# Opening and gate: fewer matmuls of ones, gate chunks copied and normalised by ScalarE, four modulation columns moved

## The chip, the cores and the metric

The kernel runs on one core of one Trainium2 chip. The metric is device time in microseconds (us) of one execution, from the first to the last instruction with what lies around them. In the text PE is the matmul engine (TensorE), DVE is VectorE, ACT is ScalarE, POOL is GpSimd and SP is SyncE, which issues most of the transfers.

## The reference

What is computed is a trunk of two layers over 512 tokens with 1024 features. Every layer has two modulated sublayers; the six modulation vectors of a layer are a matrix product with the conditioning vector. The even layer is the one that the change is in:

```python
def spatial_gating(z, ln_v_g, w_sp, b_sp):
    u, g = jnp.split(jax.nn.gelu(z), 2, axis=-1)
    bsz, length, _ = g.shape
    g = g.reshape(bsz, length // CHUNK, CHUNK, A_GROUPS, A_GROUP_DIM)
    g = layernorm(g, ln_v_g.reshape(A_GROUPS, A_GROUP_DIM))
    s = jnp.einsum('gpq,bnqgc->bnpgc', w_sp, g) + b_sp.T[:, :, None]
    return u * s.reshape(bsz, length, A_W)
...
    a = spatial_gating(z, ln_v_g, w_sp, b_sp)
    b = neighborhood_attention(split_heads(q), split_heads(k), split_heads(v), kc, vc, rpb)
    y = jnp.concatenate([a, b], axis=-1) @ w_out
...
        m = (sc_c @ w_mod[l] + b_mod[l])[:, None, :]
        sh1, s1, g1, sh2, s2, g2 = jnp.split(m, 6, axis=-1)
        h = modulate(rmsnorm(x, norm_g[l, 0]), sh1, s1)
...
        x = x + g1 * y
        x = x + g2 * sq_relu_mlp(modulate(rmsnorm(x, norm_g[l, 1]), sh2, s2), w_ff1[l], w_ff2[l])
```

Everything is in 32-bit floating point. There are four chunks of 128 tokens and four groups of 128 gate features, so the gate is normalised in 16 blocks of 128x128.

## The kernel before

Weights come in tiles of 1 MB (`raw`). ACT casts each piece of a tile to a rounded high part (L148, `whi`), and DVE or POOL subtracts for the low part (L143, `wlo`). A product of a weight and an activation is then three matmuls: high by high, high by low, low by high (L88 to L90 for a block alone, L221 to L224 for two blocks in `together`). All results go to eight PSUM banks that are handed out in a ring (`bank`); a matmul that takes a bank waits until the last reader of its former content is done. Scratch tiles come from a ring of six (`slot`). Each engine executes its instructions in the order in which the code is written, so an instruction that waits holds all that stands behind it on its engine.

**Opening.** `keep_warm(n, cols)` (L403) issues n matmuls of ones into a spare bank (L406); each is two passes on PE. It is called with ten of 512 columns. Behind them PE forms the column sums of x squared (L415): ACT squares a block of x (L420), DVE adds two blocks (L422), and PE sums each pair over the partitions, four pairs in all. All later work needs these sums.

**Attention and gate.** The loop over units u of the attention goes over pairs. For a pair it writes the scores (L885; DVE adds the bias and takes the maximum in L898, ACT exponentiates in L902), the weighing of the pair before (L931, with the sums broadcast in L939, copied by ACT in L943 and multiplied by DVE in L945), and seven steps of a filler (`more`). `turn` transposes the probabilities (L915) and ACT copies them out (L917, `pt`). The filler's parts are the value tokens (transposes copied by ACT to `vtok` in L692 and L693), the projections, the gate and the spatial product:

- `gate(i)` multiplies the tokens with one weight tile, chunk by chunk, 128x256 each (L802 to L804). For each chunk `gelu2` runs: ACT squares the chunk out of PSUM (L778), DVE multiplies by it (L779), ACT applies Tanh (L781), DVE multiplies again (L782, `gn`). DVE reads the chunk in PSUM in L779 and in L782. Then come the statistics of two blocks (L815, L816).
- `gate_norm(i)` adds epsilon to eight variances (L826, `gsd`), POOL raises them to a power (L827), and two steps later eight `tensor_scalar` (L833) normalise the eight blocks: on POOL for i=0, on DVE for i=1.
- `spatial` multiplies the normalised blocks with the spatial weights (L842), and DVE adds the bias (L845).

Behind the loop the u blocks are computed: one by L88 to L90, two by `together` (L221 to L224), with their own GELU.

**Modulation columns.** A column of the modulation is one DVE instruction over 128x1024 (L596, `gemv`). It stands in a queue from which `work` takes one. Of the first 24 columns each has its half tile (512 KB) loaded by a DMA that ACT issues (`early_load`, L581); from column 24 on whole tiles of 1 MB are loaded by SP (`gemv_load`, L589). In the attention loop each pair of units takes three columns, at steps 0, 2 and 5. `more` also makes one low part of the weights at each step, on POOL (`W.pieces(1, pool)`).

**Behind the attention** the tile of x is loaded by SP (L1047) and the first residual adds `g1 * y` to it on DVE (L1051).

## Time and profile before

| | us |
|---|---|
| median of 3 runs | 1169.52 |
| lowest and highest run | 1166.28, 1169.98 |
| the profiled execution | 1169.07 |
| its span | 1167.3 |
| PE busy | 1153.0 (99%) |
| DVE busy | 721.1 (62%) |
| ACT busy | 474.0 (41%) |
| POOL busy | 163.7 (14%) |

The span runs from the first to the last instruction that the profiler recorded; the time of the execution has 1.8 us more around it. Busy is the time in which an engine executed something. PE's share of 99% means that it seldom waits; matmuls are pipelined, and it says nothing of whether each of them was needed or ran at the full clock.

### The profile page before, as it was taken

The page shows a single profiled execution, that of the slowest core. Times are in us where ns is not written, and L with a number is a line of the kernel's source. Part 1 is how long each engine was busy: PE and PEld are TensorE (multiplying, and loading weights), DVE is VectorE, ACT ScalarE, POOL GpSimd, SP SyncE. Part 2 cuts the span into 40 slices and gives each one's busy share as a digit, 9 for nine tenths or more (in the row PEclk, how much of TensorE's full clock was granted, in tenths as well). Part 3 has the DMA queues.
Part 4 walks back from the last instruction along what each step waited for, and adds up shares of the span by engine and source line. Part 5 has one row for each costly group of instructions (what it writes and reads, how often), then busy time and mean ns, then how long its engine had stood idle before and what let it go on. Part 6 is the DMA issues. An engine that isn't in the chain of part 4 may idle for free.

```text
span 1167.3 us, 16568 instructions
## 1 busy us (share of the span) xinstructions
PE 1153.0 (99%) x6620; PEld 960.2 (82%) x6620; DVE 721.1 (62%) x1257; ACT 474.0 (41%) x939; POOL 163.7 (14%) x157
## 2 busy tenths in 40 slices
PE   9999999999999999999999999999999999999997
PEld 5788888789888888888889766799888888888887
DVE  3865778758765665666667869577743443443545
ACT  4564455546431432422336232575641331331423
POOL 0051226533000000000023120143200000000001
PEclk9999999999999999999999999999999999999999
DMA  9624543351564554554541444303232232232222
GB/s 371 244 91 145 172 163 113 123 216 38 216 214 150 213 215 153 209 216 156 204 145 42 147 112 141 105 26 120 72 109 85 96 108 93 88 108 77 104 73 72
DMA packets 32333, 161.91 MB, mean 139 GB/s; under 512 B 4416, under 2 KB 8000, under 8 KB 16256
## 3 DMA queue, kind: packets, MB, share of 16 engines
q1 hardware_dynamic: 28224, 146.43, 36.0%
q10 hardware_dynamic: 4032, 14.42, 3.7%
q8 instruction: 52, 0.85, 0.3%
q14 instruction: 25, 0.20, 0.1%
HBM read 152.52 MB, written 2.10 MB: 132 GB/s over the span
## 4 chain that ended last, share of the span: by engine, by line
PE 92%; DVE 5%; ACT 2%; DMA 1%; issue 1%; ACTq 0%; DVEq 0%; POOL 0%; POOLq 0%
PE ps L88 23%; PE ps L89 23%; PE ps L90 23%; PE ps L224 4%; PE ps L221 4%; PE ps L222 4%; PE ps L1310 3%; PE ps L491 2%; PE ps L406 1%; PE ps L931 1%; DMA graw<-in_wmB_dram 1%; DVE graw L596 1%; PE ps L885 1%; PE ps L455 1%; PE ps L915 1%
## 5 line engine op out<-in xcount | busy, mean ns | idle before, releaser
L148 ACT CAST whi<-raw 128x512 fp32r<-128x512 f32 x340 | 191.5, 616 | 198.1 <-PE ps L90 145.7
L88 PE MATMUL ps<-hhi,whi 128*128 128x512 f32 x608 | 238.4, 392 | 1.4 <-DVE gn L782 1.4
L89 PE MATMUL ps<-hhi,wlo 128*128 128x512 f32 x608 | 236.7, 389 | 0.0
L90 PE MATMUL ps<-hlo,whi 128*128 128x512 f32 x608 | 236.7, 389 | 0.0
L143 DVE TENSOR_TENSOR wlo<-raw,whi 128x512 fp32r<-128x512 f32 x285 | 195.1, 721 | 33.8 <-ACT whi L148 32.8
L90 PE MATMUL ps<-hid,whi 128*128 128x512 f32 (+1 forms) x520 | 196.3, 378 | 0.0
L89 PE MATMUL ps<-hid,wlo 128*128 128x512 f32 (+1 forms) x520 | 196.3, 378 | 0.0
L88 PE MATMUL ps<-hid,whi 128*128 128x512 f32 (+1 forms) x520 | 196.3, 378 | 0.0
L1051 DVE SCALAR_TENSOR_TENSOR x<-ps,mod,x 128x512 f32<-128x512 f32 (+1 forms) x94 | 62.7, 669 | 157.5 <-PE ps L90 147.9
L143 POOL TENSOR_TENSOR wlo<-raw,whi 128x512 fp32r<-128x512 f32 x55 | 81.0, 1490 | 426.2 <-ACT whi L148 426.1
L88 PEld LDWEIGHTS ps<-hhi,whi 128*128 128x128 f32 x608 | 114.1, 188 | 28.3 <-issue 3.2
L90 PEld LDWEIGHTS ps<-hlo,whi 128*128 128x128 f32 x608 | 114.1, 188 | 23.9
L89 PEld LDWEIGHTS ps<-hhi,wlo 128*128 128x128 f32 x608 | 114.2, 188 | 22.9
L596 DVE CUSTOM_DVE_ANT_0 graw<-graw,cB,vec 128x1024 f32<-128x1024 f32 x80 | 106.1, 1328 | 16.8 <-DMA graw<-in_wmB_dram 16.8
L88 PEld LDWEIGHTS ps<-hid,whi 128*128 128x128 f32 x520 | 97.8, 188 | 18.3
L89 PEld LDWEIGHTS ps<-hid,wlo 128*128 128x128 f32 x520 | 97.8, 188 | 18.1
L90 PEld LDWEIGHTS ps<-hid,whi 128*128 128x128 f32 x520 | 97.8, 188 | 18.0
L1186 DVE TENSOR_TENSOR z<-z 128x512 f32<-128x512 f32 (+1 forms) x72 | 46.8, 657 | 93.4 <-ACT z L1184 93.3
L1184 ACT ACTIVATE z<-ps 128x512 f32<-128x512 f32 (+1 forms) x72 | 38.9, 550 | 138.5 <-PE ps L90 136.3
L1190 DVE TENSOR_TENSOR hid<-z,hid 128x512 fp32r<-128x512 f32 (+1 forms) x72 | 45.7, 641 | 43.3 <-ACT hid L1188 43.3
L1188 ACT CAST hid<-z 128x512 fp32r<-128x512 f32 (+1 forms) x72 | 40.6, 572 | 52.2 <-DVE z L1186 52.2
L1540 POOL TENSOR_TENSOR o<-o,rstd 128x256 f32<-128x256 f32 x2 | 1.9, 950 | 321.7 <-DVE rstd L362 321.7
(267 smaller groups left out, 1733.3 us busy)
## 6 DMA issues: line engine op xcount, KB each, us to landing
raw<-in_w_ff_dram SPq DMA_DIRECT2D x64, 1024.0 KB
graw<-in_wmB_dram SPq DMA_DIRECT2D x28, 1024.0 KB
graw<-in_wmB_dram ACTq DMA_DIRECT2D x24, 512.0 KB
raw<-in_w_pw_dram SPq DMA_DIRECT2D x12, 1024.0 KB
raw<-in_w_in_dram SPq DMA_DIRECT2D x8, 1024.0 KB
wmA<-in_wmA_dram SPq DMA_DIRECT2D x7, 1024.0 KB
y<-ypad SPq DMA_DIRECT2D x90, 67.5 KB
raw<-in_w_out_dram SPq DMA_DIRECT2D x4, 1024.0 KB
```

The costliest lines, as they stand in the source:

```text
L88: pe.matmul(ps, w[0], a[0], start=first, stop=False)
L89: pe.matmul(ps, w[1], a[0], start=False, stop=False)
L90: pe.matmul(ps, w[0], a[1], start=False, stop=last)
L143: (e or dve).tensor_tensor(lo.parts[q], src, hi.parts[q].bitcast(F32), op=ALU.subtract)
L148: act.copy(hi.parts[q], src)
L221: pe.matmul(ps, w[0][:, k, c : c + P], a[0], start=n == 0, stop=False)
L222: pe.matmul(ps, w[1][:, k, c : c + P], a[0], start=False, stop=False)
L224: pe.matmul(ps, w[0][:, k, c : c + P], a[1], start=False, stop=n == len(ks) - 1)
L596: dve.tensor_tensor_reduce(out=wv, in0=wv, in1=cB, scale=1.0, scalar=vcol(V_BMOD, l * 48 + q * 8 + j % 8), op0=ALU.mult, op1=ALU.add, accu ...
L1051: dve.scalar_tensor_tensor(x[:, m, t0:t1], ps, gate[:, m : m + 1], x[:, m, t0:t1], op0=ALU.mult, op1=ALU.add)
L1186: dve.tensor_tensor(z, z, z, op=ALU.mult)
L1190: dve.tensor_tensor(lo, z, hi.bitcast(F32), op=ALU.subtract)
```

## The change

**Opening.** `keep_warm` gets five matmuls in place of ten, and one more stands behind the column sums of the second pair (k = 3).

On PE at the start of the program the rows were (`ps_127` is the spare bank, `sq` the squares):

```order
L406 MATMUL ps_127<-ones 128x512 x10
L415 MATMUL ps_140<-ones,sq_143 128x128 x4
L415 MATMUL ps_140<-ones,sq_152 128x128 x4
L415 MATMUL ps_140<-ones,sq_161 128x128 x4
L415 MATMUL ps_140<-ones,sq_170 128x128 x4
L455 MATMUL ps_212<-graw_86,sc_125 32x512 x4
```

and are now:

```order
L406 MATMUL ps_127<-ones 128x512 x5
L415 MATMUL ps_135<-ones,sq_138 128x128 x4
L415 MATMUL ps_135<-ones,sq_147 128x128 x4
L406 MATMUL ps_127<-ones 128x512
L415 MATMUL ps_135<-ones,sq_157 128x128 x4
L415 MATMUL ps_135<-ones,sq_166 128x128 x4
L457 MATMUL ps_208<-graw_86,sc_125 32x512 x4
```

Five of the matmuls of ones are gone ahead of the sums, and one stands between the second and the third pair.

**Gate chunk.** ACT copies each chunk of 128x256 from PSUM into the second half of the scratch tile before it squares it; Square and both DVE multiplications then read the copy. The bank is free after ACT's copy instead of after L782.

**Normalisation.** A small DVE instruction forms `gnb`, minus mean times the power of the variance (128x8). Eight ACT activations (Identity with scale and bias by pointer, 128x128) take the place of the eight `tensor_scalar`, for both i, with the loop over e outside and over n inside. Lines shift: L692 of before is L695 now, L778 is L782, L902 is L911, L917 is L926, and the new activations are L843.

On ACT, at the first batch (around the `vtok` copies, with the first chunk of `gate(1)` ahead), the rows were:

```order
L148 CAST whi_1879<-raw_1435 128x512
L778 ACTIVATE gelu_1896<-ps_1865 128x256
L148 CAST whi_1879<-raw_1435 128x512
L692 COPY vtok_1909<-ps_1910 128x512
L693 COPY vtok_1909<-ps_1911 128x384
L943 COPY rs_1963<-ps_1954 128x512
L902 ACTIVATE s_1967,tot_1921<-s_1967,st_1968 128x512
L902 ACTIVATE s_1971,tot_1921<-s_1971,st_1972 128x512
```

and are now:

```order
L816 COPY gelu_1896<-ps_1865 128x256
L782 ACTIVATE gelu_1896<-gelu_1896 128x256
L843 ACTIVATE gn_1637<-gn_1637,gnb_1900,gsd_1862 128x128
L843 ACTIVATE gn_1730<-gn_1730,gnb_1900,gsd_1862 128x128
L843 ACTIVATE gn_1774<-gn_1774,gnb_1900,gsd_1862 128x128
L843 ACTIVATE gn_1849<-gn_1849,gnb_1900,gsd_1862 128x128
...
L148 CAST whi_1879<-raw_1431 128x512
L695 COPY vtok_1912<-ps_1913 128x512
L696 COPY vtok_1912<-ps_1914 128x384
L952 COPY rs_1966<-ps_1957 128x512
L911 ACTIVATE s_1970,tot_1924<-s_1970,st_1971 128x512
```

The eight new activations (the four rows left out have the names of the four shown) stand between the Square of the chunk and the copies to `vtok`, behind which the sums' copy and the exponentials come.

On ACT, at the second batch (last exponential of the last pair to the last copies of the probabilities), the rows were:

```order
L902 ACTIVATE s_2198,tot_1921<-s_2198,st_2199 128x512
L148 CAST whi_2149<-raw_1739 128x512
L581 DMA graw_817<-in_wmB_dram 128x1024
L148 CAST whi_2149<-raw_1739 128x512 x2
L917 COPY pt_2244<-ps_2239 128x512
L917 COPY pt_2251<-ps_2246 128x512
L581 DMA graw_817<-in_wmB_dram 128x1024
L917 COPY pt_2267<-ps_2262 128x512
L917 COPY pt_2274<-ps_2269 128x512
```

and are now:

```order
L911 ACTIVATE s_2200,tot_1924<-s_2200,st_2201 128x512
L843 ACTIVATE gn_1637<-gn_1637,gnb_2210,gsd_2141 128x128
L843 ACTIVATE gn_1730<-gn_1730,gnb_2210,gsd_2141 128x128
L843 ACTIVATE gn_1774<-gn_1774,gnb_2210,gsd_2141 128x128
L843 ACTIVATE gn_1849<-gn_1849,gnb_2210,gsd_2141 128x128
...
L148 CAST whi_2151<-raw_1737 128x512 x3
L926 COPY pt_2246<-ps_2241 128x512
L926 COPY pt_2253<-ps_2248 128x512
L926 COPY pt_2267<-ps_2262 128x512
L926 COPY pt_2274<-ps_2269 128x512
```

The eight activations (four shown) stand behind the exponentials, the two DMA issues (L581) are gone, and the three casts of the weights stand ahead of the probability copies.

**Modulation columns.** The first 20 columns instead of 24 go by half tiles. In the loop the pairs u = 12 and 14 take one column each, at step 5, in place of three. Columns 20 to 23 come behind the attention, out of whole tiles that SP loads: 20 and 21 at the last two k steps of `together` for the u blocks 2 and 3, 22 and 23 at k steps 4 and 6 of the first residual. SP issues one whole tile ahead of the loads of x.

**Low parts.** From `begin(gate_norm(1))` on, `more` makes the low parts on DVE instead of POOL.

The diff, cut to its core:

```diff
-    keep_warm(10, 512)
+    keep_warm(5, 512)
...
             column_sums(sq, k == 1, k == KC - 1)
+            if k == 3:
+                keep_warm(1, 512)
...
-    gpool = [None, 12]
+    NE = 20
+    gpool = [None, NE // 2]
...
-        if j < 24:
+        if j < NE:
             b = j % 2 * D
             act.dma_start(early[0][:, b : b + D], I["wmB"][j // 2][:, b : b + D])
...
-        if j < 22:
+        if j < NE - 2:
             soon.append([3, lambda: early_load(j + 2)])
-        elif j == 23:
+        elif j == NE - 1:
             gemv_load(gpool[1])
...
-    def gelu2(dst, ps, n):
-
-        t = slot(cols=n, s="gelu")
+    def gelu2(dst, ps, n, t=None):
+
+        if t is None:
+            t = slot(cols=n, s="gelu")
         act.activation(t, ps, AF.Square, scale=math.sqrt(0.044715))
...
-            def rest(gt=gt, ps=ps, n=n):
-                yield from gelu2(gt, ps, 256)
+            t = slot(s="gelu")
+            act.copy(t[:, 256:], ps)
+
+            def rest(gt=gt, t=t, n=n):
+                yield from gelu2(gt, t[:, 256:], 256, t[:, :256])
...
-        for n in range(4):
-            for e in range(2):
+        nb = small(8, "gnb")
+        dve.scalar_tensor_tensor(nb.rearrange("p (n e) -> p n e", e=2), gmv[:, :, 2 * i : 2 * i + 2, 0], -1.0,
+                                 sd.rearrange("p (n e) -> p n e", e=2), op0=ALU.mult, op1=ALU.mult)
+        for e in range(2):
+            for n in range(4):
                 g = 2 * i + e
-                (dve if i else pool).tensor_scalar(gn[n][:, g * P : (g + 1) * P], gn[n][:, g * P : (g + 1) * P],
-                                  gmv[:, n, g, 0:1], sd[:, 2 * n + e : 2 * n + e + 1],
-                                  op0=ALU.subtract, op1=ALU.mult)
+                act.activation(gn[n][:, g * P : (g + 1) * P], gn[n][:, g * P : (g + 1) * P], AF.Identity,
+                               scale=sd[:, 2 * n + e : 2 * n + e + 1], bias=nb[:, 2 * n + e : 2 * n + e + 1])
...
+        low_by[0] = dve
         yield from spatial((0, 1))
...
-            W.pieces(1, pool)
+            W.pieces(1, low_by[0])
...
-            if n in (0, 2, 5):
+            if n in ((0, 2, 5) if u < 12 else (5,)):
                 work(1)
...
+    queue_gemv(NE, 24)
+
+    def hook(n):
+        if 0 < n < 7:
+            operand((4, 5, 6, 7, 0, 1)[n - 1])
+        if n > 5:
+            work(1)
...
-    evs = together([(0, w, 0), (1, w, P)], y, res, ks=order, hook=lambda n: W.pieces(n % 2, "both"))
+    evs = together([(0, w, 0), (1, w, P)], y, res, ks=order,
+                   hook=lambda n: (W.pieces(n % 2, "both"), work(n in (4, 6))))
```

## Rows read from the trace of the kernel before

**Rows 1.** The page, part 4: the chain that ended last, by engine.
```profile
PE 92%; DVE 5%; ACT 2%; DMA 1%; issue 1%; ACTq 0%; DVEq 0%; POOL 0%; POOLq 0%
```

**Rows 2.** What PE waited for: line, releaser; us in total, times, longest.
```profile
PE ps L88 <- DVE gn L782: 1.4, 1, 1.4
...
PE ps L885 <- DVE gn L782: 1.0, 1, 1.0
...
PE ps L931 <- ACT pt L917: 0.7, 1, 0.7
```

**Rows 3.** Timeline of PE, opening: start, us, engine, line, operation, out<-in, count [idle <-releaser].
```profile
0.99 11.13 PE L406 MATMUL ps<-ones 128*128 128x512 f32 x20 [0.99 <-POOL expo L314]
11.96 3.73 PE L415 MATMUL ps<-ones,sq 128*128 128x128 f32 x32
```

**Rows 4.** Timeline of PE's weight loads, opening.
```profile
4.57 0.34 PEld L406 LDWEIGHTS ps<-ones 128*128 128x128 f32 x1 [0.52 <-issue]
5.42 0.29 PEld L406 LDWEIGHTS ps<-ones 128*128 128x128 f32 x1 [0.52 <-issue]
5.95 0.19 PEld L406 LDWEIGHTS ps<-ones 128*128 128x128 f32 x1 [0.24 <-issue]
6.38 0.19 PEld L406 LDWEIGHTS ps<-ones 128*128 128x128 f32 x1 [0.24 <-issue]
```

**Rows 5.** Timeline of ACT, opening.
```profile
8.63 1.67 ACT L420 ACTIVATE sq<-x 128x512 f32<-128x512 f32 x3 [0.59 <-DMA x<-in_xT_dram]
13.05 0.63 ACT L420 ACTIVATE sq<-x 128x512 f32<-128x512 f32 x1 [2.75 <-PE ps L415]
```

**Rows 6.** Timeline of DVE, opening.
```profile
9.81 0.69 DVE L422 TENSOR_TENSOR sq<-sq,sq 128x512 f32<-128x512 f32 x1 [1.04 <-ACT sq L420]
```

**Rows 7.** Windows: us, busy by engine (x instructions), PE's granted clock, DMA share, GB/s.
```profile
10.00:20.00 10.00, 10.00 (x67) 6.35 (x67) 4.24 (x13) 2.88 (x6) 0.00 (x0) 1.00 1.01 397
```

**Rows 8.** Timeline of ACT, attention: the first vtok copy.
```profile
172.50 0.59 ACT L692 COPY vtok<-ps 128x512 f32<-128x512 f32 x1
```

**Rows 9.** Timeline of DVE, attention: variance and epsilon of the first batch.
```profile
172.65 0.17 DVE L826 TENSOR_SCALAR gsd<-gmv 128x8 f32<-128x8 f32 x1
```

**Rows 10.** Timeline of POOL, attention: the two powers.
```profile
172.90 2.60 POOL L827 TENSOR_TENSOR gsd<-gsd,expo 128x8 f32<-128x8 f32 x1 [7.81 <-DVE gsd L826]
...
194.08 1.67 POOL L827 TENSOR_TENSOR gsd<-gsd,expo 128x8 f32<-128x8 f32 x1 [6.33 <-DVE gsd L826]
```

**Rows 11.** Timeline of PE, attention: first gate matmul of the second weights.
```profile
175.39 0.39 PE L802 MATMUL ps<-whi,hhi 128*128 128x256 f32 x1
```

**Rows 12.** Lines L502, L1428 on ACT, by form: ns min/median/max, first and last start.
```profile
L502 ACT ACTIVATE hhi<-x,modA,gsA x8: 800/808/819, 20.9 to 45.4; 128x512 fp32r<-128x512 f32 x8
...
L1428 ACT ACTIVATE zc<-zc,vec x16: 597/601/603, 754.6 to 777.9; 128x256 f32<-128x256 f32 x16
```

**Rows 13.** Timeline of ACT, attention: casts and probability copies.
```profile
198.28 1.65 ACT L148 CAST whi<-raw 128x512 fp32r<-128x512 f32 x3
...
204.65 1.07 ACT L917 COPY pt<-ps 128x512 f32<-128x512 f32 x2 [3.76 <-DVE mod L596]
```

**Rows 14.** Timeline of DVE, attention: the second batch.
```profile
197.67 5.31 DVE L833 TENSOR_SCALAR gn<-gn,gmv,gsd 128x128 f32<-128x128 f32 x8
```

**Rows 15.** Timeline of PE, end of the attention: first u block.
```profile
207.66 0.50 PE L88 MATMUL ps<-hhi,whi 128*128 128x512 f32 x1
```

**Rows 16.** Windows at the end of the kernel, columns as in rows 7.
```profile
1162.00:1163.00 1.00, 0.00 (x0) 0.00 (x0) 1.00 (x4) 0.00 (x0) 0.69 (x2) 0.87 0.43 133
1163.00:1164.00 1.00, 0.00 (x0) 0.00 (x0) 0.27 (x1) 0.00 (x0) 0.00 (x0) 0.50 1.00 329
```

**Rows 17.** The page, part 5: busy, mean ns | idle before, releaser.
```profile
L143 DVE TENSOR_TENSOR wlo<-raw,whi 128x512 fp32r<-128x512 f32 x285 | 195.1, 721 | 33.8 <-ACT whi L148 32.8
...
L596 DVE CUSTOM_DVE_ANT_0 graw<-graw,cB,vec 128x1024 f32<-128x1024 f32 x80 | 106.1, 1328 | 16.8 <-DMA graw<-in_wmB_dram 16.8
```

**Rows 18.** Timeline of DVE, first residual: x<-ps.
```profile
238.17 1.41 DVE L1051 SCALAR_TENSOR_TENSOR x<-ps,mod,x 128x512 f32<-128x512 f32 x2 [6.30 <-DMA x<-in_xT_dram]
```

More of the change, by code (lines that the diff above doesn't have):

```diff
@@ L594, in gemv @@
         l, q = gemv_srcs[j // 8]
-        wv = (early[0] if j < 24 else gemv_tile[i])[:, e * D : (e + 1) * D]
+        wv = (early[0] if j < NE else gemv_tile[i])[:, e * D : (e + 1) * D]
         dve.tensor_tensor_reduce(
@@ L598, in gemv @@
             op0=ALU.mult, op1=ALU.add, accum_out=mods[(l, q)][:, j % 8 : j % 8 + 1])
-        if j < 22:
+        if j < NE - 2:
             soon.append([3, lambda: early_load(j + 2)])
-        elif j == 23:
+        elif j == NE - 1:
             gemv_load(gpool[1])
             gpool[1] += 1
-        elif e and j > 23:
+        elif e and j >= NE:
             del gemv_tile[i]
@@ L961, in body @@
     early_load(1)
-    queue_gemv(0, 24)
+    queue_gemv(0, NE)
     gate_in = {}
+    low_by = [pool]
     def filling():
@@ L980, in body @@
     fill = filling()
-    nfill = [0]
     def more(n):
@@ L985, in more @@
             begun = len(staged)
-            if next(fill, 1) is None:
-                nfill[0] += 1
+            next(fill, 1)
             stage(begun)
@@ L1027, in operand @@
         split(y[k][0], y[k][1], yb[k - 4] if k > 3 else sg[k], el=pool if k % 2 else dve)
+    queue_gemv(NE, 24)
[4 more added lines that the diff above has]
+            work(1)
     w = W.use()
-    evs = together([(2, w, 0), (3, w, P)], h, evac_u, hook=lambda n: operand((4, 5, 6, 7, 0, 1)[n - 1]) if 0 < n < 7 else None)
+    evs = together([(2, w, 0), (3, w, P)], h, evac_u, hook=hook)
     W.free()
```

## The prediction

> **What bounds the kernel now.** I read the chain of waits first: PE carries 92% of it, DVE 5%, ACT 2% [rows 1]. So only what makes PE start earlier, do less or wait less can move the end. The list of PE's waits comes next, since it prices what can be had. In the attention three of its entries belong to code the change touches: 1.4 and 1.0 us for L782, where DVE reads a gate chunk out of PSUM for the last time and so keeps the bank that PE wants, and 0.7 us for the copies of the probabilities (L917) [rows 2]. That is 3.1 us. The third view is the timeline of the opening, where PE runs matmuls of ones (L406) for 11.13 us and only then reaches the column sums (L415), 32 passes in 3.73 us [rows 3]. The sums end at 15.69 and everything after hangs on them. PE is never idle there, so the list of waits can't show this cost; the timeline does.
>
> All below is in the frame of the profiled execution, 1169.07 us. The median of the runs is 0.45 above it, less than the spread of the three runs, and is left aside. About 0.3% (3.5 us) is what a measurement of this kernel can tell from no change.
>
> **Opening: fewer matmuls of ones.** One L406 instruction is two passes (x20 for ten). Their weight loads show two rates: 0.85 us apart up to 5.42, then 0.43 [rows 4]. The removed ones are the late ones, so each pass is worth 0.43, not 11.13 / 20. With five instructions the ten passes end at 12.12 - 10 x 0.43 = 7.82. A column sum takes 3.57 / 32 = 0.112 a pass (11.96 to the last start), eight for each k pair, 0.90. Walk: the sums for k=1 run 7.82 to 8.72. The sums for k=3 end at 9.66, the new instruction of ones (two passes) at 10.52. For k=5 the DVE sum is ready at 9.81 + 0.69 = 10.50 [rows 6], so PE goes on to 11.42. For k=7 the eighth Square had waited at 13.05 for PE to release its slot [rows 5]; now the slot is free when the seventh ends at 8.63 + 1.67 = 10.30. Square 0.63, DVE sum 0.69 with its start: 11.7, and PE 11.7 to 12.6, with the pipeline's tail 12.7. Against 15.69 that is **3.0 us earlier**. What could come late next is a transfer: the 16 DMA engines are full from 10 to 20 us (share 1.01) [rows 7], and the modulation weights are consumed right behind. PE waited for no DMA here before; in the worst case I give back 1.0 us of the gain, and one more pass of ones' worth (0.43) may come on top: 2.0 to 3.4.
>
> **Gate chunk copied by ACT.** The copy of 128x256 frees the bank earlier, and DVE then reads SBUF. The two waits for L782, 1.0 and 1.4 us, go. The copy lengthens a chunk's ACT to DVE chain by about 0.45 (128x512 takes 0.59 [rows 8], and shorter forms are not half).
>
> **Normalisation on ACT, the first batch.** Before, POOL did eight L833 and nobody waited long. Now eight activations stand on ACT in one row, ahead of the cast and of the two vtok copies (L692, L693), and they wait for gnb, which waits for POOL's power (L827). The engine runs in its order, so vtok waits too. And PE's first gate matmul of the next part writes the bank that the first vtok copy reads. Before, that copy ran at 172.50 [rows 8] and PE started the matmul at 175.39 [rows 11].
> Now step by step. gsd starts at 172.65 [rows 9], or up to 0.45 later. The power took 2.60 the first time and 1.67 the second [rows 10]; it starts 0.25 behind gsd. So it ends between 172.90 + 1.67 = 174.6 and 173.35 + 2.60 = 175.95; gnb adds 0.25. An L843 of 128x128 with scale and bias by pointer has no row. The nearest are the 128x512 form, 0.808, and the 128x256 form, 0.601 [rows 12]; by the line through them 128 columns take 0.50. Activations in a row overlap: three Squares of 0.63 took 1.67, so a next one starts 0.11 before the last ends, a step of 0.39. Eight: 0.50 + 7 x 0.39 = 3.2. Bounds: 2.9 with a step of 0.35, 4.0 without overlap. Then a cast, 0.5, and the copy, 0.59. The copy ends between 174.85 + 4.3 = 179.2 and 176.2 + 4.3 = 180.5; middle 179.9. PE would be there at 175.39 - 1.0 (the wait at L885 that goes) = 174.4. So **PE stands idle about 5.5 us**, and starts the gate matmul 4.5 us late (3.8 to 5.1).
>
> **How much of it reaches the end of the attention.** From there on PE had 1.4 of waiting for L782, which goes, so it comes 3.1 late to the second spatial part. The second gnb stands on DVE where the eight L833 began at 197.67 [rows 14], thus at about 200.8. ACT: eight L843 to 204.0, three casts (1.65 for three before), then four pt copies at 1.07 for two [rows 13], the last ending about 207.6. Before, it ended at 204.65 + 1.07 = 205.72, because ACT had waited 3.76 behind a modulation column. PE began the next matmul of 128x512 at 207.66, 1.94 behind that copy [rows 15]. So now 209.4: the attention ends **1.7 us later** (0.9 to 2.5). The removed L833 of DVE (5.31) and three moved columns are therefore not a gain of PE: eight activations have taken their place on ACT, and the 3.1 us of old waits are already used up in this sum.
>
> **What the idle stretch does to PE's clock.** The trace has no PE gap of 5 us with work behind it. [...] What a restart costs is shown by the opening: passes at 0.85 instead of 0.43 up to 5.42, 4.4 us at half rate, so 2.2 us lost. I take most of it, 1.7, since ACT's queue paces part of what follows; bounds 0 and 2.2.
> [...]
>
> **The rest.** Low parts of four plus four weights go from POOL to DVE. They take 0.72 each there [rows 17], and PE waited for none of these parts: nothing. The four moved columns: 20 and 21 run while PE does the 128x512 matmuls of the u blocks, and 22 and 23 lie in the 6.30 us for which DVE is idle ahead of L1051 at 238.17 [rows 18]: hidden. If that cover were gone, 1.33 each [rows 17], 2.7 us for such a pair. SP issues one more whole load ahead of the x loads; x is what ended those 6.30 us, so it could come late by the time of 1 MB. I cost it at 0, with 0.5 as the bad end, since the load is issued long before. The extra row for gnb is small (0.2).
>
> **Sum, the forecast.** 1169.07 - 3.0 + 1.7 + 1.7 = **1169.5 us**.
>
> **The rivals.** First, the stall comes but the clock stays high: 1169.07 - 3.0 + 1.7 = 1167.8. For it: in the whole trace the column of granted clock falls only at the end, after the work. Against it: there it fell as soon as PE had run dry.
> Second, the change does what its form suggests: the power and the eight activations pass quickly, or the vtok copies find slack that I don't see, so that PE doesn't stand. Then both gains come: 1169.07 - 3.0 - 3.1 = 1163.0, **faster**. Against it is the row order of ACT; for it, that the old normalisation and columns held ACT for 3.76 us, which goes.
> Third, **slower**: the clock falls in the stall and stays at half rate for more than the opening needed, since the matmuls behind it are short and come with waits for ACT. Half rate costs half of its duration. To come out beyond 1172.6 the attention must lose 6.6 us, of which 1.7 is the stall, so 4.9 by the clock, that is 10 us at half rate, 2.2 times the opening's 4.4. I put such a case at 1169.07 - 3.0 + 1.7 + 5.5 = 1173.3. Against it: the next part has some 29 us of nearly dense matmuls.
> A fourth, that the opening gives nothing because a transfer ends the wait, would put the forecast at 1172.5; I give it little and count it with the third.
>
> **How the numbers follow.** Forecast 0.40, clock stays 0.28, no stall 0.18, slower (with the fourth) 0.14. Faster by over 0.3% means below 1165.6: all of the no-stall case and some of the lower tail of the second, 0.22. Slower means beyond 1172.6: the third and a tail of the forecast, 0.16. The rest, 0.62, is within 0.3%. The range for 8 in 10 goes from 1163.5 (the forecast and the clock case with their bounds: 1169.07 - 3.4 + 0.9 = 1166.6, then into the no-stall case, of which half stays out) to 1172.5 (1169.07 - 2.0 + 2.5 + 2.2 + 0.5 = 1172.3).
>
> **What would show it.** In the new timeline: L415 ends near 12.7; if it ends near 15 the opening's step is wrong. In the attention the list of PE's waits has a gate matmul held for 5 to 6 us by the vtok copy; if no wait above 2 us stands there, the second rival is right. Matmuls of 128x256 right behind it that start twice as far apart as those of before at 175.39 would show the fall of the clock. The first matmul of the u block (207.66 before) should come, counted from the end of L415, 1.7 to 3.4 later than it did. What would make me wrong is a quicker power or L843, or DVE or PE waiting for the moved loads.

## The result and the profile after

| | before | after |
|---|---|---|
| median, us | 1169.67 (9 runs, 1166.28 to 1170.78) | 1173.3 (9 runs, 1171.94 to 1174.64) |
| ratio to before | | 1.0034, 95% interval 1.0023 to 1.0044 |
| the profiled execution, us | 1169.07 | 1172.26 |
| its span, us | 1167.3 | 1170.5 |
| PE busy, us | 1153.0 | 1151.3 |

The change makes the kernel slower by 3.6 us by the medians, 3.2 by the two profiled executions. The forecast was 1169.5, with a range up to 1172.5: about no change was expected, and the median lies 0.8 beyond the range. The profiled execution lies 1.0 below the median.

Read one after the other, the views of after show where the time went. First the opening, in PE's timeline (columns as in rows 3):

```profile
0.99 7.29 PE L406 MATMUL ps<-ones 128*128 128x512 f32 x10 [0.99 <-POOL expo L314]
8.11 1.96 PE L415 MATMUL ps<-ones,sq 128*128 128x128 f32 x16
9.91 1.02 PE L406 MATMUL ps<-ones 128*128 128x512 f32 x2
10.77 1.95 PE L415 MATMUL ps<-ones,sq 128*128 128x128 f32 x16
```

The sums end at 10.77 + 1.95 = 12.72, against 15.69 before [rows 3]: 2.97 us won, the size that was worked out. Then the list of PE's waits (line, releaser; us in total, times, longest):

```profile
PE ps L806 <- ACT vtok L695: 7.8, 1, 7.8
...
PE ps L224 <- DVE ylo L94: 0.7, 1, 0.7
```

Both waits for L782, 1.4 and 1.0 us, and the one for the probability copies, 0.7 [rows 2], are gone. In their place stands one of 7.8 us, where a gate matmul waits for the vtok copy, and a new one of 0.7 us for a low part of y. The timeline of ACT shows the first one's make-up:

```profile
170.32 0.42 ACT L782 ACTIVATE gelu<-gelu 128x256 f32<-128x256 f32 x1
175.01 3.18 ACT L843 ACTIVATE gn<-gn,gnb,gsd 128x128 f32<-128x128 f32 x8 [4.27 <-DVE gnb L838]
178.10 0.60 ACT L148 CAST whi<-raw 128x512 fp32r<-128x512 f32 x1
178.61 0.57 ACT L695 COPY vtok<-ps 128x512 f32<-128x512 f32 x1
```

After the Square (170.32) ACT is idle for 4.27 us until gnb is there, runs the eight activations in 3.18, casts, and only at 178.61 copies vtok. DVE and POOL in the same stretch, gsd and gnb on DVE, the power and a low part of the weights on POOL:

```profile
170.87 0.17 DVE L833 TENSOR_SCALAR gsd<-gmv 128x8 f32<-128x8 f32 x1
...
173.76 1.21 DVE L838 SCALAR_TENSOR_TENSOR gnb<-gmv,gsd 128x8 f32<-128x8 f32 x1 [1.19 <-POOL gsd L834]
```

```profile
171.12 2.61 POOL L834 TENSOR_TENSOR gsd<-gsd,expo 128x8 f32<-128x8 f32 x1 [7.74 <-DVE gsd L833]
173.70 1.26 POOL L143 TENSOR_TENSOR wlo<-raw,whi 128x512 fp32r<-128x512 f32 x1
```

And PE's timeline when it is released, with the slices of 3 us around it (columns as in rows 7; the granted clock is the third column from the end):

```profile
179.23 0.58 PE L806 MATMUL ps<-whi,hhi 128*128 128x256 f32 x1 [7.79 <-ACT vtok L695]
179.61 0.41 PE L807 MATMUL ps<-whi,hlo 128*128 128x256 f32 x1
179.82 0.41 PE L808 MATMUL ps<-wlo,hhi 128*128 128x256 f32 x1
```

```profile
172.00:175.00 3.00, 0.00 (x0) 0.00 (x0) 1.79 (x4) 0.00 (x0) 2.95 (x2) 0.79 0.04 16
175.00:178.00 3.00, 0.00 (x0) 0.00 (x0) 0.00 (x0) 2.99 (x8) 0.00 (x0) 0.50 0.00 0
178.00:181.00 3.00, 1.77 (x8) 1.77 (x9) 0.94 (x2) 2.03 (x5) 1.27 (x1) 0.50 0.00 0
181.00:184.00 3.00, 3.00 (x16) 3.00 (x16) 2.19 (x8) 2.60 (x7) 0.00 (x0) 0.50 0.01 3
184.00:187.00 3.00, 3.00 (x28) 3.00 (x27) 2.02 (x6) 2.59 (x8) 1.76 (x2) 1.00 0.17 30
```

PE is empty from 172 to 179. The granted clock is 0.79 and then 0.50 in these slices, and back at 1.00 in the one from 184. Behind the wait matmuls start 0.21 apart, and 0.12 apart once the clock is back (184.06 and 184.18). At the end of the attention the first u block starts here:

```profile
209.26 0.50 PE L88 MATMUL ps<-hhi,whi 128*128 128x512 f32 x1
```

Before, it was 207.66 [rows 15]. Counted from the end of the sums it comes at 209.26 - 12.72 = 196.54, before at 207.66 - 15.69 = 191.97: the stretch up to the end of the attention is 4.57 us longer. From there to the last matmul the changed kernel loses another 1.6 us: 1.0 at the low part of y and behind it, and 0.6 in the depthwise convolution near 742 us. The sum, -2.97 + 4.57 + 1.6 = 3.2, is the difference of the spans. All of this compares one execution of each kernel.

### The profile page after: what moved, and what is told of

Same layout as the page of the kernel before. It is cut to its first block, busy times and chain, and to the rows that moved or that the text cites. A ratio compares the mean times of both kernels' runs of the same rounds, so it can differ in the third digit from the quotient of the medians.

```text
span 1170.5 us, 16535 instructions
## 1 busy us (share of the span) xinstructions
PE 1151.3 (98%) x6612; PEld 959.1 (82%) x6612; DVE 725.2 (62%) x1259; ACT 483.1 (41%) x963; POOL 145.9 (12%) x141
## 4 chain that ended last, share of the span: by engine, by line
PE 92%; DVE 4%; ACT 2%; issue 1%; DMA 0%; POOL 0%; DVEq 0%; ACTq 0%; POOLq 0%
PE ps L88 23%; PE ps L90 23%; PE ps L89 23%; PE ps L1328 3%; PE ps L224 3%; PE ps L221 3%; PE ps L222 3%; PE ps L493 2%; PE ps L940 1%; PE ps L924 1%; PE ps L894 1%; PE ps L406 1%; PE ps L457 1%; DVE ylo L94 1%; DMA graw<-in_wmB_dram 0%
## 5 line engine op out<-in xcount | busy, mean ns | idle before, releaser
L143 DVE TENSOR_TENSOR wlo<-raw,whi 128x512 fp32r<-128x512 f32 x293 | 200.1, 720 | 37.4 <-ACT whi L148 36.5
L143 POOL TENSOR_TENSOR wlo<-raw,whi 128x512 fp32r<-128x512 f32 x47 | 69.4, 1488 | 425.3 <-ACT whi L148 423.7
L343 ACT ACTIVATE sq<-x 128x256 f32<-128x256 f32 (+1 forms) x41 | 20.3, 496 | 64.3 <-DVE x L1068 64.2
```

Of the source, the lines that this page charges most:

```text
L143: (e or dve).tensor_tensor(lo.parts[q], src, hi.parts[q].bitcast(F32), op=ALU.subtract)
```

## The experiments

Each run is timed beside the kernel before on the same chip; these stood at 1169.61, 1169.44 and 1169.86 us in the three groups. An offset is the start of a matmul in a run's timeline less the start of the same matmul in the one timeline of before; a minus sign means earlier.

### The opening alone

```diff
-    keep_warm(10, 512)
+    keep_warm(5, 512)
...
             column_sums(sq, k == 1, k == KC - 1)
+            if k == 3:
+                keep_warm(1, 512)
```

> The kernel before with the change of the opening alone. My theory: the opening gives what it did in the trace of after, where every PE instruction from the column sums to the attention starts 3.02 us earlier, and nothing downstream takes it back; so 3.0 us less than before, a ratio of 0.9974. The rival, that the gain is lost again further down because the attention or a transfer sets the end: a ratio of 1.000, with the offset against before going back to zero in the attention.

Measured: 1167.68 us, ratio 0.9985 (0.9976 to 0.9994). It is a gain, but of 1.9 us and not of 3.0. In its profile the matmuls behind the opening are 2.46 us early up to the attention and 3.04 behind it (a part of that is the wait at L887, 1.0 before as L885 and 0.65 here), and 1.2 is lost in the convolution, which leaves 1.9. So what is won in the opening is still there behind the attention; where it is lost is the convolution. The opening itself differs from one execution to the next. Timelines of PE and ACT:

```profile
8.17 2.20 PE L415 MATMUL ps<-ones,sq 128*128 128x128 f32 x16 [0.57 <-DVE sq L422]
```

```profile
6.26 2.17 ACT L420 ACTIVATE sq<-x 128x512 f32<-128x512 f32 x4
9.10 2.19 ACT L420 ACTIVATE sq<-x 128x512 f32<-128x512 f32 x4 [0.67 <-DMA x<-in_xT_dram]
```

PE now waits 0.57 us for the sum of the first pair: its matmuls of ones end sooner than in after (0.99 + 6.61 = 7.60 against 8.28), and ACT's Squares begin later, at 6.26 (after: 5.95). The second four Squares wait 0.67 us for x. With ten matmuls of ones that was hidden: PE reached the sums at 11.96. So the ones were what held the sums before, and behind them the loads of x have a say in when the opening ends.

### The first batch back on POOL

```diff
+        if i == 0:
+            for n in range(4):
+                for e in range(2):
+                    pool.tensor_scalar(gn[n][:, e * P : (e + 1) * P], gn[n][:, e * P : (e + 1) * P],
+                                       gmv[:, n, e, 0:1], sd[:, 2 * n + e : 2 * n + e + 1],
+                                       op0=ALU.subtract, op1=ALU.mult)
+            return
         nb = small(8, "gnb")
```

> The changed kernel with the first batch of the normalisation back on POOL (eight L833 as before) and only the second on ACT. My theory, that eight activations ahead of the vtok copies make the 7.8 us wait: no PE wait above 1.5 us is left in the attention, the clock stays high there, and the time falls to about 1166 to 1168 us, ratio to before 0.996 to 0.999, like the run in which the activations stand one step later on ACT. The rival, that the copies of the chunks or the low parts on DVE make the wait: a wait of 5 us or more stays and the time stays above 1171.

Measured: 1165.30 us, ratio 0.9965 (0.9953 to 0.9978): 8.0 us below the changed kernel, and 4.1 below the kernel before. What is left of PE's waits in the attention:

```profile
PE ps L947 <- ACT pt L933: 0.4, 1, 0.4
...
PE ps L806 <- ACT vtok L695: 0.3, 1, 0.3
```

Nothing above 0.4 us. So the wait of 7.8 us comes from the first batch on ACT, and everything else in the change together is a gain: 4.1 us by the medians, of which the opening alone gave 1.9.

### The first batch one step later on ACT

```diff
         yield
         yield
+        if i == 0:
+            yield
         nb = small(8, "gnb")
```

> The changed kernel with one more step between the power and the first eight activations, so that they stand on ACT behind the two vtok copies, the sums' copy and the exponentials of the next pair. My theory: the 7.8 us wait of PE is the place in ACT's row, not the work of the activations. So no PE wait above 1 us is left there, the granted clock stays at 1.00, and the attention ends earlier than in the kernel before by the 3 us of old waits or a part of them, instead of 4.6 later: 5 to 7.5 us less than the changed kernel, 1166 to 1168 us, a ratio to before of 0.996 to 0.998. The rival, that eight activations on ACT cost PE as much wherever they stand, since ACT has no room in the attention: the wait moves to the probability copies or to the spatial product, and the time stays within 1.5 us of the changed kernel's 1173.3.

Measured: 1168.11 us, ratio 0.9987 (0.9978 to 0.9996), 5.2 below the changed kernel and 0.1 above the expected stretch. The wait for vtok has shrunk to 0.3, with the same eight activations on ACT; what made the long wait was their place. But no wait above 1 us and a clock of 1.00 were expected too, and that was missed:

```profile
PE ps L926 <- ACT s L913: 2.1, 1, 2.1
...
PE ps L806 <- ACT vtok L695: 0.3, 1, 0.3
```

PE waits 2.1 us, from 191.4 to 193.5, for the exponentials of the last pair: DVE comes late to their scores. Here the clock falls too, in slices of 2 us:

```profile
192.00:194.00 2.00, 0.52 (x3) 0.52 (x4) 2.00 (x7) 1.39 (x4) 0.44 (x1) 0.88 0.00 0
194.00:196.00 2.00, 2.00 (x9) 1.90 (x8) 1.15 (x4) 2.00 (x8) 0.00 (x0) 0.50 0.03 8
196.00:198.00 2.00, 2.00 (x11) 1.59 (x11) 0.00 (x0) 2.00 (x6) 0.00 (x0) 0.77 0.00 0
```

The run with the first batch on POOL differs from this one in that batch alone. There the wait for the same exponentials is 0.3, and the time is 2.8 us lower. So of the 8.0 us that the first batch on ACT costs, 5.2 are its place, and 2.8 are left in the later place: the rival was right in a part.

### The chunk copies alone

```diff
+            t = slot(s="gelu")
+            act.copy(t[:, 256:], ps)
...
-            def rest(gt=gt, ps=ps, n=n):
-                yield from gelu2(gt, ps, 256)
+            def rest(gt=gt, t=t, n=n):
+                yield from gelu2(gt, t[:, 256:], 256, t[:, :256])
```

> The kernel before with the copy of the gate chunks by ACT alone, everything else as before. By the list of PE's waits both waits for L782 (1.0 and 1.4 us) go. If PE's waits are independent of each other: 2.4 us less than before, ratio 0.998. The rival: the chunk's chain is longer by the copy (0.4 us four times a part) and PE waits for the exponentials or the spatial product instead; the time is within 1 us of before, ratio 0.999 to 1.001.

Measured: 1169.20 us, ratio 0.9997 (0.9988 to 1.0006), no change. The two waits for L782 are gone, and in the list of PE's waits stands instead

```profile
PE ps L919 <- ACT s L906: 1.7, 1, 1.7
```

a wait for the exponentials of the last pair. In this one profile the first u block starts 1.48 us earlier than before, of which 0.45 was there ahead of the attention: 1.0 is left of the 2.4, and the medians don't show even that clear of noise. DVE, with three columns in each pair, is late to the scores anyway.

### Opening, copies and second batch, nothing moved

The kernel before with the opening's edit, the copies, and the new normalisation for i = 1 only:

```diff
+        if i:
+            nb = small(8, "gnb")
+            dve.scalar_tensor_tensor(nb.rearrange("p (n e) -> p n e", e=2), gmv[:, :, 2 * i : 2 * i + 2, 0], -1.0,
+                                     sd.rearrange("p (n e) -> p n e", e=2), op0=ALU.mult, op1=ALU.mult)
...
+            return
         for n in range(4):
             for e in range(2):
                 g = 2 * i + e
-                (dve if i else pool).tensor_scalar(
+                pool.tensor_scalar(
```

> The kernel before with the opening's change, the chunk copies, and the second batch of the normalisation on ACT; the first batch stays on POOL, all 24 columns and the low parts stay where they were. If the three add up: the opening 1.9 us (as measured alone), the copies up to 2.4, the second batch up to 0.7 for the probability copies: 1164.6 to 1166 us, ratio 0.996 to 0.997, faster than any run so far. The rival: the second batch on ACT delays the probability copies by more than the columns did (in the changed kernel they come from 205.3 on, 5 us behind the last exponential), so that the copies' gain is lost: 1167 to 1168.

Measured: 1166.05 us, ratio 0.9972 (0.9963 to 0.9982), at the upper end of the first expectation, with the wait of 1.7 us for the exponentials still there. By the ratios that is some 1.5 us below the opening alone, with all 24 columns in the loop (the intervals just overlap). Against the run with the first batch on POOL (1165.30) it lacks the moved columns and low parts; they make 0.75 us by the medians, and the intervals overlap. The profiles show why it is little. From the start of the attention to the first u block after it, this run gains 1.6 us against before, and the one with columns and low parts moved 3.1, of which 1.0 is lost again at the low part of y.

### The late batch with all 24 columns in the loop

```diff
-    NE = 20
+    NE = 24
...
-            if n in ((0, 2, 5) if u < 12 else (5,)):
+            if n in (0, 2, 5):
                 work(1)
```

(with the later calls for the four columns taken out)

> The changed kernel with the first eight activations one step later on ACT (as in the earlier run) and with all 24 columns where they were before. It tells what the move of the four columns is worth once the long wait is gone. My theory: the move costs more than it gives, since PE's wait of 0.7 us for the low part of y comes from columns 20 and 21; but three columns in each of the last pairs make DVE late to the scores of the last pair, where PE already waits 2.1 us for the exponentials. I expect about no change against 1168.1, between 1167 and 1169.5: no wait for ylo, a longer one (3 us or more) for the exponentials. The rival, that the move is a gain by itself: 1170 or more.

Measured: 1171.41 us, ratio 1.0015 (1.0006 to 1.0024). The rival was right: moving the columns is worth 3.3 us beside the late batch (1168.11 with them moved). PE's waits:

```profile
PE ps L926 <- ACT s L913: 2.3, 1, 2.3
...
PE ps L896 <- ACT pt L928: 1.9, 1, 1.9
```

The wait for the low part of y is gone, as expected, but a new one of 1.9 us for the probability copies has come, beside 2.3 for the exponentials. Behind the wait of 1.9 the granted clock is 0.59 and 0.56 in the slices from 186 to 190, so a part of the 3.3 us is the clock's. The copies start at 185.91, behind a Tanh (L785) for which ACT waits 2.6 us, until DVE has done a column (1.65 us) and the multiplication of the chunk (1.47).

### Matmuls of ones in the stretch of the wait

```diff
             pr = bank()
+            if u == 11:
+                for _ in range(8):
+                    pe.matmul(pr, ones, ones.unsqueeze(1).to_broadcast([P, 4, P]), start=True, stop=True)
```

> The changed kernel with eight more matmuls of ones (16 passes of 0.43, 6.9 us) ahead of the broadcast of the sums at the end of pair 2, which is just where PE runs dry; they write the bank that the broadcast writes next. They compute nothing that is used. PE still has to wait for the vtok copy, until the same moment, but is busy for most of the time. My theory: the clock's fall costs about 2.1 us (the offset against before grows from +3.8 to +5.9 over the gate matmuls behind the wait, at half rate). So the granted clock stays 1.00, the gate matmuls run at full rate, and the time is about 2 us less than the changed kernel's, 1171.3, a ratio to before of 1.0015. The rival: what PE loses at half rate is covered by ACT's queue, which sets the end of the attention anyway; the time stays at 1173.3 within 0.5 us.

Measured: 1172.75 us, ratio 1.0031 (1.0019 to 1.0043). That is 0.55 below the changed kernel: the 2 us of the first expectation were not there, and the rival (within 0.5) is nearer. In its profile the offset at the start of the attention is -2.15, in that of after -3.02, so the opening had won 0.9 less there. It was run again beside the changed kernel:

> The changed kernel once more, beside the two runs that are compared with it. As before: 1173.3 within 1 us, PE's wait for the vtok copy 7.8 us.

> The changed kernel with eight matmuls of ones in the stretch where PE waits for the vtok copy, beside the changed kernel itself. In the profile of the first such run the matmuls behind the wait stood 2.1 us earlier, counted from the end of the opening, and the end of the attention 1.3 us earlier. My theory, that the clock's fall costs 1.3 us of the end: 1.3 us less than the changed kernel in this comparison (0.8 to 2.1). The rival, that it costs nothing at the end: within 0.5 us.

Measured: the changed kernel 1173.12 us, ratio 1.0029 (1.0017 to 1.0040); with the ones 1172.23, ratio 1.0024 (1.0014 to 1.0034). The difference of the medians is 0.9 us, inside what was expected, and the intervals overlap, so by the times alone it is weak. The profile is plain. PE's wait for vtok, the slices from 175 to 184, and the first gate matmuls:

```profile
PE ps L806 <- ACT vtok L695: 0.7, 1, 0.7
```

```profile
175.00:178.00 3.00, 3.00 (x8) 1.09 (x6) 0.61 (x1) 2.35 (x7) 0.59 (x1) 1.00 0.00 0
178.00:181.00 3.00, 2.27 (x26) 1.98 (x26) 0.29 (x1) 2.68 (x7) 1.28 (x1) 1.00 0.00 0
181.00:184.00 3.00, 3.00 (x27) 3.00 (x26) 2.84 (x9) 1.96 (x5) 0.00 (x0) 1.00 0.03 8
```

```profile
179.88 0.39 PE L806 MATMUL ps<-whi,hhi 128*128 128x256 f32 x1 [0.73 <-ACT vtok L695]
180.10 0.28 PE L807 MATMUL ps<-whi,hlo 128*128 128x256 f32 x1
180.22 0.28 PE L808 MATMUL ps<-wlo,hhi 128*128 128x256 f32 x1
```

The release comes at the same moment (179.88; in the second run of the changed kernel 179.87), with the clock at 1.00 and matmuls 0.12 apart. The first u block then starts at 208.58 instead of 209.62 in that run: of the clock's price of 2.1 about 1.0 us reaches the end of the attention. The rest is lost where PE, now earlier, meets ACT's row: it waits 0.23 for a probability copy at 205.24, and the copies pace the matmuls behind it.

### Low parts on DVE from the first power on

```diff
         yield from gate(0)
+        low_by[0] = dve
         begin(gate_norm(0))
         yield from gate(1)
         begin(gate_norm(1))
-        low_by[0] = dve
```

> The changed kernel with the low parts of the weights on DVE from the first power on, instead of from the second, so that POOL does none while DVE forms gnb. In the changed kernel gnb took 1.21 us where a DVE instruction of 128x8 takes 0.17, with a low part of 1.26 us on POOL at the same time. My theory, that the two engines hold each other up there: gnb takes about 0.2, the activations begin 1.0 us earlier, PE's wait shrinks from 7.8 to about 6.8, and the time by 0.5 to 1.0. The rival, that gnb is slow for a reason of its own (its operands with steps of 2 and 8): gnb stays at 1.2 and the wait at 7.8 or more.

Measured: 1171.26 us, ratio 1.0014 (1.0006 to 1.0023), 1.9 below the changed kernel in the same group, twice what was expected (the two intervals overlap in part). On DVE, on POOL, and PE's wait:

```profile
173.35 0.17 DVE L838 SCALAR_TENSOR_TENSOR gnb<-gmv,gsd 128x8 f32<-128x8 f32 x1
```

```profile
171.26 2.05 POOL L834 TENSOR_TENSOR gsd<-gsd,expo 128x8 f32<-128x8 f32 x1 [7.74 <-DVE gsd L833]
```

```profile
PE ps L806 <- ACT vtok L695: 6.2, 1, 6.2
```

gnb takes 0.17 in place of 1.21, and the power 2.05 in place of 2.61. In the changed kernel POOL's low part had started at 173.70, 0.06 ahead of gnb, and gnb ended with it: 173.76 + 1.21 = 174.97, and 173.70 + 1.26 = 174.96. The wait is 6.2, which is 1.6 less; 1.0 of that is gnb's and 0.5 the power's.

### The four columns later

```diff
     def hook(n):
         if 0 < n < 7:
             operand((4, 5, 6, 7, 0, 1)[n - 1])
-        if n > 5:
-            work(1)
...
-        chunk(2 + i, w, i * P, y, res, 0, order, el="both")
+        chunk(2 + i, w, i * P, y, res, 1.2, order, el="both")
```

> The changed kernel with modulation columns 20 and 21 moved out of the last two steps of the u blocks into the first residual, and 22 and 23 from there to its two following blocks. My theory: on DVE columns 20 and 21 (1.27 and 2.30 us) stand ahead of the GELU of the last u blocks, make it 3 us late, and PE waits for the low part of y (0.66 us, 0.95 with the slower matmuls behind it). So that wait goes and the time is about 1.0 us less than the changed kernel's, 1172.3, a ratio to before of 1.0025. The rival, that the four low parts of weights on DVE (2.49 us) ahead of the operands' low parts make them late: PE still waits 0.5 us or more for ylo and the time doesn't change. A third: DVE comes late to the first residual and the gain is given back there.

Measured: 1177.13 us, ratio 1.0068 (1.0055 to 1.0081), 3.8 above the changed kernel. The cause of the small wait was right: PE waits no more for the low part of y, and its offset stays flat there. What set the time was the third expectation, that DVE comes late to the first residual, at a far higher price. SP's queue and DVE:

```profile
237.37 0.33 SPq L592 DMA_DIRECT2D graw<-in_wmB_dram  x1
```

```profile
247.05 1.29 DVE L599 CUSTOM_DVE_ANT_0 graw<-graw,cB,vec 128x1024 f32<-128x1024 f32 x1 [4.74 <-DMA graw<-in_wmB_dram]
...
248.26 0.75 DVE L1066 SCALAR_TENSOR_TENSOR x<-ps,mod,x 128x512 f32<-128x512 f32 x1
```

The load of the second whole tile, which holds columns 22 and 23, is issued only when column 21 has been read (237.37; in the changed kernel at 229.47). Column 22 waits for it until 247.05, and the next residual addition stands behind it at 248.26; the casts of the next weights stand behind that on ACT, and PE waits 2.5 us for them, with the clock down once more (0.75 and 0.68 in the slices of 3 us from 250).

### Column 20 at the first step

From the kernel with the first batch on POOL:

```diff
-        if n > 5:
+        if n in (0, 7):
             work(1)
```

> The kernel with the first batch back on POOL (1165.3), with column 20 at the first k step of the u blocks instead of the second to last; column 21 stays at the last. If the two columns in one place make PE wait 0.6 us for the low part of y: one of them is taken out of the way, the GELU of the last u blocks is 1.3 us earlier, the wait goes and the time is 0.5 to 0.9 less, 1164.5. The rival: the earlier column delays the low parts of the first operands instead and the wait stays 0.5 or more.

Measured: 1165.90 us, ratio 0.9969 (0.9957 to 0.9981), no gain over 1165.30, and the wait of 0.6 us stays. The rival was right:

```profile
213.37 2.33 DVE L599 CUSTOM_DVE_ANT_0 graw<-graw,cB,vec 128x1024 f32<-128x1024 f32 x1
...
219.61 2.31 DVE L599 CUSTOM_DVE_ANT_0 graw<-graw,cB,vec 128x1024 f32<-128x1024 f32 x1
```

Both columns take 2.3 us there, where the first of the two took 1.27 when they stood together. (In the changed kernel the column of 2.30, from 227.13, ran beside a low part on POOL of 226.95 to 228.35, and the one of 1.27, from 225.93, almost wholly ahead of it.) So nothing is won: the GELU of the last u blocks starts at 221.85, against 222.39 with both columns in one place, and PE's matmuls there are 0.5 earlier as well.

## Why the prediction was wrong

**What the miss is made of.** The forecast was 1169.5 in the frame of the profiled execution, and that came out at 1172.26. Of the 2.8 us between them 1.2 lie in the attention (3.4 put, 4.57 measured), 1.0 at the low part of y (put at nothing) and 0.6 in the convolution (not in the sum). The median is 1.0 higher still; a part of that is an opening that on most executions wins less than 3.0.

**Opening: right in the profile, too large in the median.** The walk gave 12.7 for the end of the sums and the trace has 12.72. That the two agree so well is in part luck: the ones ended 0.5 later than put (8.28 against 7.82), because their passes became faster only at 6.83 and not at 5.95, while the last pair, for which the walk had PE wait until 11.7, was ready at 11.47, and PE ran through without a wait. And the second profile of the changed kernel is 2.48 us early at the start of the attention, those of the ten other runs with this opening 2.15 to 2.88, and the edit alone was worth 1.9 by the medians. The term took the loads of x as they fell in the one trace of before, where PE came so late that their spread could not be seen. The lower bound, 2.0, covers all the profiles; the 1.9 of the edit alone lies just below it.

**The first batch: the mechanism was right, the wait too small.** This is the step that failed first: the sum that gave the end of the vtok copy. The predicted chain is the one in the trace: gsd, power, gnb, eight activations, cast, vtok copy, gate matmul. Eight activations were put at 3.2 and took 3.18. The wait was put at 5.5, at a copy's end of 179.9; it is 7.8, and the release at 179.23 is 182.2 in the frame of before (2.97 added). Three terms of the sum were mis-sized. gsd stands at 170.87, so 173.9 in that frame, 1.2 later than in before [rows 9] where "up to 0.45" was allowed: the copies delay each chunk of the chain, and the chunks follow each other (with the copies alone gsd stands at 173.44, with no shift of PE). The power took 2.61, the time that rows 10 have for this same batch (2.60), where the middle between it and the second batch's was taken, 0.5 less. And gnb took 1.21 where 0.25 was put: the low part on POOL ran beside it, and with that gone it took 0.17. By the middle of the forecast's bounds the three make about 1.0, 0.5 and 1.0, of which 0.1 comes back behind them.

**What reaches the end of the attention.** Put at 1.7 for the wait and 1.7 for the clock, 3.4; measured 4.57. The two runs with matmuls of ones give its parts: about 1.0 by the clock, the rest by the wait. So the wait's share is some 3.5, twice what was put. The row of ACT that the forecast walked for the end came true in its lengths, with the eight activations and the casts ahead of the four probability copies:

```profile
205.31 2.01 ACT L926 COPY pt<-ps 128x512 f32<-128x512 f32 x4
```

The first u block starts 1.94 behind the last of them, as was put. But they end at 207.32, which is 210.3 in the frame of before, where 207.6 was put: the whole row came 2.7 late. The release, 2.3 later than put, is most of that; that the clock makes the rest is argued and not shown. That a wait with work behind it lowers the clock no row of before shows; the 1.7 was an estimate from the opening's passes alone [rows 4]. The clock did fall, as the forecast assumed, to 0.50, and behind the wait it cost 2.1 us (the offset against before grows from 3.8 to 5.9 over the first gate matmuls), close to the opening's 2.2. But half of it was slack against ACT's row. So the third rival's time came true, 1173.3, by luck and not by its mechanism: it wanted 10 us at half rate, and the clock was back at 1.00 after 5. One reading in the forecast was off: at the end of the kernel before, the clock did not fall as soon as PE had run dry. PE's last matmul ended at 1160.69, and the slice from 1161 to 1162 still shows 1.00; 0.87 and 0.50 come in the two behind it [rows 16].

**"Hidden" was wrong for columns 20 and 21.** This is the second step that failed. They were taken to run beside the matmuls of the u blocks at no cost; 22 and 23 did, for the offset stays flat behind them. DVE of before, then DVE and PE of after:

```profile
221.21 1.77 DVE L94 TENSOR_TENSOR ylo<-sg,yhi 128x512 fp32r<-128x512 f32 x1
224.74 0.69 DVE L779 SCALAR_TENSOR_TENSOR gelu<-gelu,ps 128x512 f32<-128x512 f32 x1 [1.76 <-ACT gelu L778]
```

```profile
218.40 2.49 DVE L143 TENSOR_TENSOR wlo<-raw,whi 128x512 fp32r<-128x512 f32 x4
...
225.93 1.27 DVE L599 CUSTOM_DVE_ANT_0 graw<-graw,cB,vec 128x1024 f32<-128x1024 f32 x1
...
227.13 2.30 DVE L599 CUSTOM_DVE_ANT_0 graw<-graw,cB,vec 128x1024 f32<-128x1024 f32 x1
...
229.37 1.27 DVE L783 SCALAR_TENSOR_TENSOR gelu<-gelu,ps 128x512 f32<-128x512 f32 x2
```

```profile
235.62 0.73 PE L224 MATMUL ps<-ylo,whi 128*128 128x512 f32 x2 [0.66 <-DVE ylo L94]
```

The two columns take 1.27 and 2.30 us on DVE directly ahead of the GELU of the last u blocks, which starts at 229.37. Before, it started at 224.74, at the offset of that stretch (1.6) 226.3. The 3 us go through ACT and DVE to the low part of y, and PE waits. With the columns gone from there the wait was gone, in the run that put them later and in the one that kept all 24 in the loop. The columns are not all that is new ahead of this GELU: the four low parts of the weights (218.40) now stand on DVE too, and the last low part of y ahead of the columns starts at 224.23, 1.4 later than before at the same offset. They were put at nothing as well. Without the columns they cost PE no wait; with the columns their share of the 1.0 us was not tested.

**A part of the sum that was set at nothing.** The prediction found that columns and normalisation taken off DVE are "not a gain of PE", since the activations take their place. That holds only with the first batch ahead of vtok. With that batch one step later the moved columns were worth 3.3 us. With it on POOL the columns mattered less, 0.75 together with the low parts. The copies alone gave nothing clear of noise, but with the opening and the second batch on ACT the time was some 1.5 us below the opening's alone.

**Left open:** 0.6 us in the depthwise convolution near 742 us, where its matmuls on the second weight tile start later against before. It comes in all these runs, 0.3 to 1.9 us, with waits for ACT or for transfers that differ from run to run. All are read against one execution of before, so how much of it is that execution's own is open, and so is the cause.

## What to carry to other kernels

Work moved to an engine with idle time takes a place in that engine's row, and what matters is who stands behind it: eight short activations cost 7.8 us of PE because they waited for another engine's result ahead of a copy that frees a PSUM bank; one step later in the row that wait was 0.3, though the time stayed 2.8 us above that of the same kernel with them on POOL. Price a small instruction at the duration that the trace has for it in the same place, and look at what the other engines do at the same moment: gnb took 1.21 us beside a low part on POOL and 0.17 without. And a list of waits is not a list of gains: remove one, and the next late engine holds PE at nearly the same place.

## What the runs showed of the hardware

- PE's clock. After the wait of 7.8 us the granted clock was 0.50, and 1.00 again in the slice from 184, 5 us after the release at 179.23. Behind the release matmuls of 128x256 started 0.21 apart, and 0.12 apart from 184.06 on. With matmuls of ones in the stretch of the wait the clock stayed at 1.00, and the gate matmuls behind it (first at 179.88) started 0.12 apart from 180.10 on. The short waits go either way: behind waits of 1.9 (24 columns), 2.1 (late batch) and 2.5 us (columns later) the granted clock was down to 0.56, 0.50 (slices of 2 us) and 0.68 (slices of 3 us), and it stayed at 1.00 after waits of 1.73, 1.75 and 2.35 (second batch, copies alone, 24 columns). The length of a short wait alone doesn't tell which it was in these runs.
- At the start the moment at which the ones go from 0.85 to 0.43 us a pass is not the same in each execution: with five of them 4.29 in the first run with ones in the wait, 5.29 with the opening alone and 6.83 in the changed kernel. The column of granted clock shows 1.00 there all the while in the changed kernel, so that it is the clock that is low there was taken from the rate of the passes alone.
- DVE and POOL side by side: gnb of 128x8 took 1.21 us beside POOL's low part and 0.17 without, and it ended together with that low part (174.97 and 174.96), which had started 0.06 ahead of it. In the changed kernel a modulation column took 2.30 us at 227.13, with a low part on POOL from 226.95 on, and 1.28 at 170.95, where the power ran on POOL from 171.12 on. What makes an instruction longer beside a low part was not shown.
